# Attention scores of two key heads in one chain, their products interleaved by half of the array

## The chip, the cores and the metric

One core of a Trainium2 chip. The metric is the device time of one execution in microseconds; the time of a kernel is the median of its runs.

## What is computed

Two layers of a decoder trunk over 256 tokens of width 1024. Each layer has a gated feed-forward block, a mixing block of two branches that add up, a second feed-forward block and a small embedding block. The change is in the attention branch of the mixing block: 16 query heads and 4 key heads of width 64, a window of 128 keys, one sink logit a head. Cut to what matters:

```python
q, k = head_rmsnorm(a_q), head_rmsnorm(a_k)
scores = einsum("bnqhgd,bnkhd->bnhgqk", q, windows(k)) * 64 ** -0.5
scores = where(band & valid, scores, -inf)
mx = maximum(max(scores, axis=-1), sink)
pr = exp(scores - mx)
den = sum(pr, axis=-1) + exp(sink - mx)
ha = einsum("bnhgqk,bnkhd->bnqhgd", pr / den, windows(v))
h = h + (sigmoid(g_m) * (hm @ w_branch_m) + sigmoid(g_a) * (ha @ w_branch_a)) @ w_out
```

## The kernel before

**Precision by splitting.** Every matmul operand is a pair: a rounded part `hi`, cast by ScalarE, and the rest `lo`, subtracted by VectorE (`splitting`, L466). A product is three matmuls: hi x hi, hi x lo, lo x hi. All weights go this way: `raw` comes by DMA, `wh` and `wl` are its two parts, in a ring of 8 slots that TensorE gives back as it uses them up (`feed`, L328).

**Jobs and chains.** The matmuls with weights are jobs that run one after the other. In a mixing block they are `kvq` (keys, values and queries of the attention), `v`, `gt` (a gate), `if` (input and forget gates), `ya` (the attention's output by `w_branch_a`), then those of the other branch. All other work runs in chains: Python generators whose steps are put between the matmuls of the jobs (`tick`, L196). A planner's clock (`Clock`, L60) estimates when a step's inputs are ready, and a chain goes on when TensorE's estimated time has come to that. TensorE, ScalarE, VectorE and SyncE execute their instructions in the order that this writes; a later instruction doesn't overtake a waiting one.

**Attention.** Key heads are handled by two pairs p; g = 0 and 1 are the two key heads of a pair, whose 64 rows lie in partitions 0 to 63 and 64 to 127. `groups` (L1171) starts one chain `group` (L1184) for each p, each block t of 128 queries and each g, at most five at once. A chain does the following. A mask goes into a PSUM bank `sc` by a matmul of the full array (identity times `band`, 512 columns). On top go the score products: S = 128 (t = 0) or 256 keys (t = 1), stationary a 64 x 128 tile of `qT`, moving a 64 x S tile of `kT`. A bank holds four heads for t = 0 and two for t = 1, that is twelve or six products; t = 1 takes two banks in turn. VectorE takes the maxima `mx` (a reduction and a small step), ScalarE the exponentials `pr` with their sums `dn`. Then come `es`, the reciprocal, the scaling of `pr`, and for each block of keys four transposes into a bank `tp`, its split into `ptd`, and three matmuls `ha` (output by values). The last chain of a p and t splits `ha` into `haT`, which shares its tiles with `qT`, so the profile shows this as `qT<-ha`.

**Who waits for it.** `ya` starts when all chains have been started (L797 passes `finish(groups[0])`). It runs over the first half of `haT` (p = 0) for both halves of the output, 96 matmuls, and then over the second half (p = 1), another 96. Ahead of each step it finishes the chains that write what it reads (`XT.wait`, L158), both t. Beside it runs the chain `scans`, with VectorE steps on `gates`, five transposes of `gates` into a `tp` bank, and their copy `gcols`.

**Banks.** PSUM has eight banks; all of `kvq`, `v`, `gt`, `ya`, `sc`, `tp`, `ha` are tiles of one pool (L184). A new tile that is given a bank waits for the last reader of the tile that had it.

Of the kernel before, what the change touches and what calls it, by code (L numbers as in the profile page):

```python
# [14 lines left out]
AF = mybir.ActivationFunctionType  # L15
ALU = mybir.AluOpType
AX = mybir.AxisListType
PSUM = bass.MemoryType.PSUM

P = 128  # L20
# [10 lines left out]
AQ, AKV, AD = 16, 4, 64  # L31
# [6 lines left out]
ACTIVE = 5  # L38
# [125 lines left out]
class Trunk:  # L164
# [561 lines left out]
    def mix(self, l, xT, sink):  # L726
# [15 lines left out]
        def before():  # L742
            self.feature_columns()
            att.begin()
            groups.append(self.later(att.groups(groups)))
# [351 lines left out]
class Swa:  # L1097
# [73 lines left out]
    def groups(self, chains):  # L1171
        tr, acc = self.tr, {}
        for p in range(2):
            for t in range(NT):
                while any(self.inputs.get(i, tr) is tr or self.inputs[i] in tr.bg
                          for i in [(0, s) for s in range(t + 1)] + [(p + 1, t)]):
                    yield
                for g in range(2):
                    while sum(c in tr.bg for c in chains) > ACTIVE:
                        yield  # L1180
                    chains.append(tr.start(self.group(t, p, g, acc)))
                    self.haT.written(chains[-1], 4 * p, 4, t)

    def group(self, t, p, g, acc):  # L1184

        tr, nc = self.tr, self.nc
        S = (t + 1) * P
        per = NB // S
        rows = slice(g * AD, (g + 1) * AD)
        tok = slice(t * P, (t + 1) * P)  # L1190
        hd = slice(4 * (2 * p + g), 4 * (2 * p + g) + 4)
        pr = tr.slot("pr")[:, : 4 * S].rearrange("p (j s) -> p j s", j=4)
        mx, den, es = tr.col("mx", 4), tr.col("dn", 4), tr.col("es", 4)

        def scores(j0):
            ps = tr.bank("sc").rearrange("p (j s) -> p j s", j=per)
            mask = tr.band[:, 2 * P - S :]
            nc.tensor.matmul(ps, tr.identb, mask[:, None, :].to_broadcast([P, per, S]), start=True, stop=False,
                             skip_group_check=True)
            for j in range(per):  # L1200
                for x, y in ((0, 0), (0, 1), (1, 0)):
                    nc.tensor.matmul(ps[:, j, :], self.qT[x](4 * p + j0 + j, tok, p=rows), self.kT[rows, y, p, :S],
                                     start=False, stop=x == 1, skip_group_check=True)
            return ps

        def weights(j0, ps):
            js = slice(j0, j0 + per)
            nc.vector.tensor_reduce(mx[:, js], ps, axis=AX.X, op=ALU.max)
            nc.vector.scalar_tensor_tensor(mx[:, js], mx[:, js], -0.125, self.nsink[:, hd][:, js], op0=ALU.mult,
                                           op1=ALU.min)  # L1210
            yield
            for j in range(per):
                i = j0 + j
                nc.scalar.activation(pr[:, i, :], ps[:, j, :], AF.Exp, scale=0.125, bias=mx[:, i : i + 1],
                                     accum_out=den[:, i : i + 1])

        for j0 in range(0, 4, per):
            ps = scores(j0)
            yield
            yield from weights(j0, ps)  # L1220
        nc.vector.tensor_tensor(es, mx, self.sink[:, hd], op=ALU.add)
        yield
        nc.scalar.activation(es, es, AF.Exp)
        yield
        nc.vector.tensor_tensor(den, den, es, op=ALU.add)
        nc.vector.reciprocal(den, den)
        yield
        for j in range(4):
            nc.scalar.mul(pr[:, j, :], pr[:, j, :], den[:, j : j + 1])
        yield  # L1230
        total = 2 * (t + 1)
        for s in range(t + 1):
            ps = tr.bank("tp")
            for j in range(4):
                nc.tensor.transpose(ps[:, j * P : (j + 1) * P], pr[:, j, s * P : (s + 1) * P], tr.ident)
            yield
            ptd = tr.slot("ptd", F32R)[:, : 2 * NB].rearrange("p (x n) -> p x n", x=2)
            yield from tr.splitting(ptd[:, 0], ptd[:, 1], ps)
            yield
            if (t, p) not in acc:  # L1240
                acc[t, p] = [tr.bank("ha"), 0]
            out, n = acc[t, p]
            acc[t, p][1] += 1
            tr.mm3(out, self.vpad[s, 0][:, 2 * p + g, :], self.vpad[s, 1][:, 2 * p + g, :], ptd[:, 0], ptd[:, 1],
                   n == 0, n == total - 1)
        if n == total - 1:
            yield
            yield from tr.splitting(self.haT[0](4 * p, tok, 4), self.haT[1](4 * p, tok, 4),
                                    out.rearrange("p (j t) -> p j t", j=4))
# [28 lines left out]
```

## Time and profile before

| | us |
|---|---|
| runs before: median (lowest to highest of 3) | 1404.9 (1402.35 to 1405.91) |
| the profiled execution | 1401.73 |
| its span, first to last instruction | 1400.0 |
| TensorE busy in it | 1384.3 |
| VectorE busy | 863.0 |
| ScalarE busy | 727.8 |

Granted TensorE clock over the span: 0.999 of full. Matmuls are pipelined: a record of one lasts longer than its share of the engine, and the next starts before it ends. The pace is read from start to start, or from how many lie in a stretch. L130 stands for nearly all instructions, since one helper records them all; tiles tell them apart. `sc<-band` is a mask, `sc<-kT,qT` a score product.

### The profile page before, as it was taken

Reading aid. Unit: us, or ns where it says so; the run is one execution under the profiler, and the core shown is the slowest. Engines: PE = TensorE matmul, PEld = TensorE weight load, DVE = VectorE, ACT = ScalarE, POOL = GpSimd, SP = SyncE. Lnnn points to the kernel's source line nnn. Section 1 sums busy time; section 2 is a strip of 40 time slices with the busy share of each in tenths; the row PEclk is TensorE's granted clock in tenths of the full one; section 3 lists DMA queues with packets and bytes.
Section 4 is the critical chain, followed back from the end, with each engine's and each line's share of the span. In section 5 each row is a group of like instructions: output and inputs, shape, how many; then the busy total and the mean of one; then the engine's idle time right before and its main releaser. Section 6 shows DMA issues by size and latency. Waiting matters only on the chain.

```text
span 1400.0 us, 21954 instructions
## 1 busy us (share of the span) xinstructions
PE 1384.3 (99%) x9056; PEld 1249.0 (89%) x9056; DVE 863.0 (62%) x1213; ACT 727.8 (52%) x1138; POOL 53.8 (4%) x84
## 2 busy tenths in 40 slices
PE   8999999999999999999999999999999999999998
PEld 6999887899899889988879998878998998999886
DVE  5655457656886665454565554586668876554544
ACT  5554346765665454443554443467656654444433
POOL 0000012000000000000000000120000000000000
PEclk9999999999999999999999999999999999999999
DMA  6665645355545565565456566443545544755651
GB/s 210 221 206 172 219 147 182 107 135 169 177 151 181 166 204 188 166 232 181 149 172 210 178 198 212 143 145 117 151 151 196 175 158 161 220 190 182 203 180 60
DMA packets 125830, 243.81 MB, mean 174 GB/s; under 512 B 14977, under 2 KB 23841, under 8 KB 125730
## 3 DMA queue, kind: packets, MB, share of 16 engines
q1 hardware_dynamic: 125730, 242.41, 54.2%
q8 instruction: 71, 1.16, 0.3%
q14 instruction: 29, 0.24, 0.1%
HBM read 241.34 MB, written 1.05 MB: 173 GB/s over the span
## 4 chain that ended last, share of the span: by engine, by line
PE 93%; DMA 3%; DVE 2%; ACT 1%; issue 1%; POOL 0%; SPq 0%; ACTq 0%; POOLq 0%
PE dn L130 16%; PE pg L130 15%; PE pu L130 14%; PE gt L130 7%; PE z L130 7%; PE gu L130 6%; PE kvq L130 5%; PE ya L130 3%; PE v L130 3%; PE ym L130 3%; PE og L130 3%; PE yo L130 3%; PE tp L130 3%; PE sc L130 2%; DMA raw<-in_ffn_w_gate_dram 1%; PE ha L130 1%
## 5 line engine op out<-in xcount | busy, mean ns | idle before, releaser
L130 DVE TENSOR_TENSOR wl<-raw,wh 128x1024 fp32r<-128x1024 f32 (+1 forms) x448 | 541.5, 1222 | 372.8 <-ACT wh L130 369.3
L130 ACT CAST wh<-raw 128x1024 fp32r<-128x1024 f32 x448 | 461.8, 1049 | 432.7 <-PE dn L130 88.4
L130 PE MATMUL dn<-wh,hid 128*128 128x512 f32 x688 | 217.9, 395 | 0.0
L130 PE MATMUL pg<-uT,wh 128*128 128x256 f32 x1088 | 194.6, 282 | 0.0
L130 PE MATMUL pu<-uT,wh 128*128 128x256 f32 x1088 | 193.6, 281 | 0.0
L130 PEld LDWEIGHTS pg<-uT,wh 128*128 128x128 f32 x1088 | 167.1, 189 | 0.2
L130 PEld LDWEIGHTS pu<-uT,wh 128*128 128x128 f32 x1088 | 166.9, 189 | 0.0
L130 PEld LDWEIGHTS dn<-wh,hid 128*128 128x128 f32 x688 | 129.3, 188 | 29.8
L130 PE MATMUL pg<-uT,wl 128*128 128x256 f32 x544 | 153.2, 282 | 0.0
L130 PE MATMUL pu<-uT,wl 128*128 128x256 f32 x544 | 153.1, 281 | 0.0
L130 PE MATMUL dn<-wl,hid 128*128 128x512 f32 x352 | 139.1, 395 | 0.0
L130 PEld LDWEIGHTS pu<-uT,wl 128*128 128x128 f32 x544 | 102.7, 189 | 0.0
L130 PEld LDWEIGHTS pg<-uT,wl 128*128 128x128 f32 x544 | 102.6, 189 | 0.0
L130 PE MATMUL gt<-uT,wh 128*128 128x256 f32 x512 | 93.7, 284 | 0.0
L130 PE MATMUL z<-uT,wh 128*128 128x256 f32 x512 | 92.3, 282 | 0.0
L130 PE MATMUL gu<-wh,uT 128*128 128x512 f32 x256 | 84.3, 406 | 1.2 <-ACT uT L130 1.2
L130 PEld LDWEIGHTS gt<-uT,wh 128*128 128x128 f32 x512 | 79.0, 189 | 1.2
L130 PEld LDWEIGHTS dn<-wl,hid 128*128 128x128 f32 x352 | 66.2, 188 | 15.1
L130 PEld LDWEIGHTS z<-uT,wh 128*128 128x128 f32 x512 | 78.7, 189 | 0.2
L130 PE MATMUL z<-uT,wl 128*128 128x256 f32 x256 | 72.1, 282 | 0.0
L130 PE MATMUL gt<-uT,wl 128*128 128x256 f32 x256 | 72.0, 281 | 0.0
L130 PE MATMUL kvq<-wh,uT 128*128 128x512 f32 x192 | 63.7, 402 | 0.0
(194 smaller groups left out, 2061.5 us busy)
## 6 DMA issues: line engine op xcount, KB each, us to landing
raw<-in_w_in_dram SPq DMA_DIRECT2D x60, 1024.0 KB, 5.1
raw<-in_ffn_w_up_dram SPq DMA_DIRECT2D x40, 1024.0 KB, 5.1
raw<-in_ffn_w_down_dram SPq DMA_DIRECT2D x40, 1024.0 KB, 5.2
raw<-in_ffn_w_gate_dram SPq DMA_DIRECT2D x39, 1024.0 KB, 5.7
raw<-in_w_branch_a_dram SPq DMA_DIRECT2D x16, 512.0 KB, 6.0
raw<-in_w_branch_m_dram SPq DMA_DIRECT2D x8, 1024.0 KB, 5.0
raw<-in_w_out_dram SPq DMA_DIRECT2D x8, 1024.0 KB, 5.1
raw<-in_ple_gate_w_dram SPq DMA_DIRECT2D x8, 1024.0 KB, 6.6
```

The costliest lines, as they stand in the source:

```text
L130: return issue(*args, **kw)
```

## The change

`group` is cut in two. `scores` does for both g of a p and t what stood ahead of `es`: two banks at once, both masks, then the products in turn, one of g = 0 (rows 0 to 63), one of g = 1 (rows 64 to 127), each into its own bank; then the maxima of both, then the exponentials of both. At its end it adds two chains `outputs`, one for each g, which do the rest as before. `groups` starts a pair when fewer than five chains run, the chain `groups` itself being one of them (before: a single chain when at most five run); the pair's chain counts as two.

```diff
--- before.py
+++ after.py
@@ -1175,49 +1175,53 @@
                 while any(self.inputs.get(i, tr) is tr or self.inputs[i] in tr.bg
                           for i in [(0, s) for s in range(t + 1)] + [(p + 1, t)]):
                     yield
-                for g in range(2):
-                    while sum(c in tr.bg for c in chains) > ACTIVE:
-                        yield
-                    chains.append(tr.start(self.group(t, p, g, acc)))
-                    self.haT.written(chains[-1], 4 * p, 4, t)
-
-    def group(self, t, p, g, acc):
+                while sum(c in tr.bg for c in chains) >= ACTIVE:
+                    yield
+                chains += 2 * [tr.start(self.scores(t, p, acc, chains))]
+                self.haT.written(chains[-1], 4 * p, 4, t)
+
+    def scores(self, t, p, acc, chains):
+
 
         tr, nc = self.tr, self.nc
         S = (t + 1) * P
         per = NB // S
-        rows = slice(g * AD, (g + 1) * AD)
         tok = slice(t * P, (t + 1) * P)
-        hd = slice(4 * (2 * p + g), 4 * (2 * p + g) + 4)
-        pr = tr.slot("pr")[:, : 4 * S].rearrange("p (j s) -> p j s", j=4)
-        mx, den, es = tr.col("mx", 4), tr.col("dn", 4), tr.col("es", 4)
-
-        def scores(j0):
-            ps = tr.bank("sc").rearrange("p (j s) -> p j s", j=per)
-            mask = tr.band[:, 2 * P - S :]
-            nc.tensor.matmul(ps, tr.identb, mask[:, None, :].to_broadcast([P, per, S]), start=True, stop=False,
-                             skip_group_check=True)
+        rows = [slice(g * AD, (g + 1) * AD) for g in range(2)]
+        hd = [slice(4 * (2 * p + g), 4 * (2 * p + g) + 4) for g in range(2)]
+        pr = [tr.slot("pr")[:, : 4 * S].rearrange("p (j s) -> p j s", j=4) for _ in range(2)]
+        mx, den = ([tr.col(n, 4) for _ in range(2)] for n in ("mx", "dn"))
+        mask = tr.band[:, None, 2 * P - S :].to_broadcast([P, per, S])
+        for j0 in range(0, 4, per):
+            js = slice(j0, j0 + per)
+            ps = [tr.bank("sc").rearrange("p (j s) -> p j s", j=per) for _ in range(2)]
+            for g in range(2):
+                nc.tensor.matmul(ps[g], tr.identb, mask, start=True, stop=False, skip_group_check=True)
             for j in range(per):
                 for x, y in ((0, 0), (0, 1), (1, 0)):
-                    nc.tensor.matmul(ps[:, j, :], self.qT[x](4 * p + j0 + j, tok, p=rows), self.kT[rows, y, p, :S],
-                                     start=False, stop=x == 1, skip_group_check=True)
-            return ps
-
-        def weights(j0, ps):
-            js = slice(j0, j0 + per)
-            nc.vector.tensor_reduce(mx[:, js], ps, axis=AX.X, op=ALU.max)
-            nc.vector.scalar_tensor_tensor(mx[:, js], mx[:, js], -0.125, self.nsink[:, hd][:, js], op0=ALU.mult,
-                                           op1=ALU.min)
+                    for g in range(2):
+                        nc.tensor.matmul(ps[g][:, j, :], self.qT[x](4 * p + j0 + j, tok, p=rows[g]),
+                                         self.kT[rows[g], y, p, :S], start=False, stop=x == 1, skip_group_check=True)
             yield
-            for j in range(per):
-                i = j0 + j
-                nc.scalar.activation(pr[:, i, :], ps[:, j, :], AF.Exp, scale=0.125, bias=mx[:, i : i + 1],
-                                     accum_out=den[:, i : i + 1])
-
-        for j0 in range(0, 4, per):
-            ps = scores(j0)
+            for g in range(2):
+                nc.vector.tensor_reduce(mx[g][:, js], ps[g], axis=AX.X, op=ALU.max)
+                nc.vector.scalar_tensor_tensor(mx[g][:, js], mx[g][:, js], -0.125, self.nsink[:, hd[g]][:, js],
+                                               op0=ALU.mult, op1=ALU.min)
             yield
-            yield from weights(j0, ps)
+            for g in range(2):
+                for j in range(per):
+                    i = j0 + j
+                    nc.scalar.activation(pr[g][:, i, :], ps[g][:, j, :], AF.Exp, scale=0.125, bias=mx[g][:, i : i + 1],
+                                         accum_out=den[g][:, i : i + 1])
+        for g in range(2):
+            chains.append(tr.later(self.outputs(t, p, g, acc, hd[g], pr[g], mx[g], den[g])))
+            self.haT.written(chains[-1], 4 * p, 4, t)
+
+    def outputs(self, t, p, g, acc, hd, pr, mx, den):
+
+        tr, nc = self.tr, self.nc
+        tok = slice(t * P, (t + 1) * P)
+        es = tr.col("es", 4)
         nc.vector.tensor_tensor(es, mx, self.sink[:, hd], op=ALU.add)
         yield
         nc.scalar.activation(es, es, AF.Exp)
```

What stands in the queues, at three places of the first layer (the second layer has the same).

TensorE at the first scores, p = 0, t = 0, before (`qT_136` is the hi part, `qT_138` the lo part):

```order
L130 MATMUL kvq_2225<-wh_2144,uT_117 128x512
L130 MATMUL kvq_2225<-wl_2145,uT_117 128x512
L130 MATMUL kvq_2225<-wh_2144,uT_119 128x512
L130 LDWEIGHTS identb
L130 MATMUL sc_2315<-band,identb 128x512
L130 MATMUL sc_2315<-kT_1996,qT_136 128x128 x2
L130 MATMUL sc_2315<-kT_1996,qT_138 128x128
```

and after the change:

```order
L130 MATMUL kvq_2225<-wh_2144,uT_119 128x512
L130 LDWEIGHTS identb
L130 MATMUL sc_2317<-band,identb 128x512
L130 LDWEIGHTS identb
L130 MATMUL sc_2318<-band,identb 128x512
L130 MATMUL sc_2317<-kT_1996,qT_136 128x128
L130 MATMUL sc_2318<-kT_1996,qT_136 128x128
```

Twelve products into one bank have become 24 that change bank, and half of the array, at each step, behind two masks.

TensorE inside `ya`, before (`qT_136` and `qT_138` are the first half of `haT`, `qT_137` and `qT_139` the second):

```order
L130 MATMUL ya_3185<-qT_136,wh_2953 128x256
L130 MATMUL ya_3185<-qT_138,wh_2953 128x256
L130 MATMUL ya_3185<-qT_136,wl_2954 128x256
L130 MATMUL ha_3082<-ptd_3208,vpad_1994 128x512 x3
L130 MATMUL ya_3186<-qT_136,wh_2953 128x256
L130 MATMUL ya_3186<-qT_138,wh_2953 128x256
L130 MATMUL ya_3186<-qT_136,wl_2954 128x256
```

and after:

```order
L130 MATMUL ya_3165<-qT_136,wl_2990 128x256
L130 MATMUL ha_3229<-ptd_3253,vpad_1994 128x512 x3
L130 MATMUL ha_3229<-ptd_3255,vpad_1994 128x512 x3
L130 MATMUL tp_3340<-ident,gates_3159 128x4
L130 MATMUL tp_3340<-ident,gates_3158 128x4
L130 MATMUL tp_3340<-ident,gates_3159 128x4
L130 MATMUL tp_3340<-ident,gates_3160 128x4 x2
L130 MATMUL ya_3162<-qT_137,wh_3013 128x256
L130 MATMUL ya_3162<-qT_139,wh_3013 128x256
```

The last `ha` stood inside the first half of `ya`, with 54 matmuls of that half behind it. Now the last two stand at its end, and behind the transposes of `gates` comes the first matmul of the second half.

VectorE at the same place, before:

```order
L130 TENSOR_SCALAR nM_3184<-gates_3183 4x256
L130 TENSOR_SCALAR nM_3184<-gates_3183 4x128
L130 TENSOR_TENSOR wl_3241<-raw_3104,wh_3240 128x1024
L130 TENSOR_TENSOR qT_139<-ha_3082,qT_137 128x4x128
L130 TENSOR_TENSOR wl_3303<-raw_3104,wh_3302 128x1024
L130 TENSOR_TENSOR rows_93<-nM_3184,rows_93 4x384
L130 TENSOR_TENSOR wl_3313<-raw_3211,wh_3312 128x1024
L130 TENSOR_TENSOR wl_3338<-raw_3211,wh_3337 128x1024
L130 COPY gcols_3368<-tp_3353 128x20
```

and after:

```order
L130 TENSOR_SCALAR nM_3161<-gates_3160 4x128
L130 TENSOR_TENSOR ptd_3253<-tp_3233,ptd_3253 128x512
L130 TENSOR_TENSOR ptd_3255<-tp_3241,ptd_3255 128x512
L130 TENSOR_TENSOR wl_3301<-raw_3097,wh_3300 128x1024
L130 TENSOR_TENSOR rows_93<-nM_3161,rows_93 4x384
L130 TENSOR_TENSOR wl_3311<-raw_3221,wh_3310 128x1024
L130 COPY gcols_3346<-tp_3340 128x20
L130 TENSOR_TENSOR wl_3337<-raw_3221,wh_3336 128x1024
L130 TENSOR_TENSOR qT_139<-ha_3229,qT_137 128x4x128
L130 TENSOR_TENSOR wl_3391<-raw_3320,wh_3390 128x1024
```

The subtraction `qT<-ha` stood two places behind `nM`, with `gcols` five places later. Now `gcols` and one `wl` stand ahead of it.

TensorE at the last scores, p = 1, t = 1, inside `gt`, before:

```order
L130 MATMUL gt_2754<-uT_116,wh_2496 128x256
L130 MATMUL gt_2754<-uT_118,wh_2496 128x256
L130 MATMUL gt_2754<-uT_116,wl_2497 128x256
L130 LDWEIGHTS identb
L130 MATMUL sc_2849<-band,identb 128x512
L130 MATMUL sc_2849<-kT_1996,qT_137 128x256 x2
L130 MATMUL sc_2849<-kT_1996,qT_139 128x256
```

and after:

```order
L130 MATMUL tp_2921<-ident,pr_2636 128x128 x4
L130 MATMUL gt_2719<-uT_116,wh_2579 128x256
L130 MATMUL gt_2719<-uT_118,wh_2579 128x256
L130 MATMUL gt_2719<-uT_116,wl_2580 128x256
L130 MATMUL gt_2719<-uT_116,wh_2579 128x256
L130 MATMUL gt_2719<-uT_118,wh_2579 128x256
L130 MATMUL gt_2719<-uT_116,wl_2580 128x256
L130 LDWEIGHTS identb
L130 MATMUL sc_2939<-band,identb 128x512
L130 LDWEIGHTS identb
L130 MATMUL sc_2940<-band,identb 128x512
```

One mask has become two in a row. In the built program `sc_2939` has the bank of the transposes `tp_2908`, which stand six `gt` matmuls further up, and `sc_2940` that of `tp_2921`, the transposes shown. Before, six `gt` matmuls and an `ha` stood ahead of the mask, and no transposes.

## Rows read from the trace of the kernel before

**Rows 1.** The page: the busy time of TensorE and the shares of the chain that ended last, by engine and by line:

```profile
PE 1384.3 (99%) x9056; PEld 1249.0 (89%) x9056; DVE 863.0 (62%) x1213; ACT 727.8 (52%) x1138; POOL 53.8 (4%) x84
...
PE 93%; DMA 3%; DVE 2%; ACT 1%; issue 1%; POOL 0%; SPq 0%; ACTq 0%; POOLq 0%
PE dn L130 16%; PE pg L130 15%; PE pu L130 14%; PE gt L130 7%; PE z L130 7%; PE gu L130 6%; PE kvq L130 5%; PE ya L130 3%; PE v L130 3%; PE ym L130 3%; PE og L130 3%; PE yo L130 3%; PE tp L130 3%; PE sc L130 2%; DMA raw<-in_ffn_w_gate_dram 1%; PE ha L130 1%
```

**Rows 2.** The waits of TensorE over the whole run: who waited for whom, us in total, times, the longest. No wait of over 0.15 us is listed between 228 and 340 us:

```profile
PE tp L130 <- DVE xn L130: 4.0, 2, 2.5
...
PE tp L130 <- DVE wl L130: 1.6, 1, 1.6
...
PE tp L130 <- DVE sg L130: 1.0, 1, 1.0
```

**Rows 3.** Groups of ScalarE's instructions from 228 to 340 us (the attention stage of the first layer): line, engine, operation, tiles, shapes, count, then busy us, mean ns, idle us before them and what ended it:

```profile
L130 ACT CAST wh<-raw 128x1024 fp32r<-128x1024 f32 x28 | 29.3, 1053 | 12.4 <-DMA raw<-in_w_in_dram 5.0 <-PE ya L130 4.8 <-PE gt L130 1.3
```

**Rows 4.** TensorE in order of time around the first score blocks: start us, us to the last end, engine, line, operation, tiles, shapes, count:

```profile
233.46 0.39 PE L130 MATMUL kvq<-wh,uT 128*128 128x512 f32 x1
233.69 0.39 PE L130 MATMUL sc<-band,identb 128*128 128x512 bf16 x1
234.01 1.55 PE L130 MATMUL sc<-kT,qT 64*128 64x128 f32 x12
235.49 0.39 PE L130 MATMUL sc<-band,identb 128*128 128x512 bf16 x1
235.81 1.55 PE L130 MATMUL sc<-kT,qT 64*128 64x128 f32 x12
237.29 0.50 PE L130 MATMUL kvq<-wh,uT 128*128 128x512 f32 x1
...
238.10 0.39 PE L130 MATMUL sc<-band,identb 128*128 128x512 bf16 x1
238.42 0.97 PE L130 MATMUL sc<-kT,qT 64*128 64x256 f32 x6
239.32 0.39 PE L130 MATMUL sc<-band,identb 128*128 128x512 bf16 x1
```

**Rows 5.** The instructions that write or read the tile `sc`: count, duration in ns (min/median/max), first and last start in us, shapes:

```profile
L130 PEld LDWEIGHTS sc<-kT,qT x192: 182/187/192, 234.0 to 982.1; 64*128 64x128 f32 x192
L130 PE MATMUL sc<-kT,qT x192: 268/275/389, 234.0 to 982.3; 64*128 64x128 f32 x96, 64*128 64x256 f32 x96
...
L130 PE MATMUL sc<-band,identb x24: 389/390/391, 233.7 to 981.2; 128*128 128x512 bf16 x24
```

**Rows 6.** The instructions on the tile `gates`, the same columns: the loads of its five tiny transposes:

```profile
L130 PEld LDWEIGHTS tp<-ident,gates x10: 133/136/138, 326.6 to 1019.8; 4*128 4x128 f32 x10
```

**Rows 7.** TensorE's loads in order of time at the first of these transposes:

```profile
326.57 0.39 PEld L130 LDWEIGHTS tp<-ident,gates 4*128 4x128 f32 x5
```

**Rows 8.** TensorE in order of time inside `ya`: the last `ha`, then `ya` and the transposes of `gates`:

```profile
318.00 0.86 PE L130 MATMUL ha<-ptd,vpad 128*128 128x512 f32 x3
318.70 0.40 PE L130 MATMUL ya<-qT,wh 128*128 128x256 f32 x2
...
326.13 0.40 PE L130 MATMUL ya<-qT,wh 128*128 128x256 f32 x2
326.36 0.28 PE L130 MATMUL ya<-qT,wl 128*128 128x256 f32 x1
326.57 0.47 PE L130 MATMUL tp<-ident,gates 4*128 4x4 f32 x5
326.98 0.51 PE L130 MATMUL ya<-qT,wh 128*128 128x256 f32 x2
```

**Rows 9.** ScalarE in order of time in the same stretch: the cast that begins the split of `ha`; a cast of `ptd` has the same shape (in brackets idle us before and what ended it):

```profile
318.90 0.59 ACT L130 CAST qT<-ha 128x512 fp32r<-128x512 f32 x1 [1.33 <-PE ha L130]
```

**Rows 10.** VectorE in order of time in the same stretch:

```profile
315.60 0.69 DVE L130 TENSOR_TENSOR ptd<-tp,ptd 128x512 fp32r<-128x512 f32 x1
...
321.45 0.67 DVE L130 TENSOR_TENSOR qT<-ha,qT 128x512 fp32r<-128x512 f32 x1
...
326.23 1.23 DVE L130 TENSOR_TENSOR wl<-raw,wh 128x1024 fp32r<-128x1024 f32 x1 [1.14 <-ACT wh L130]
327.38 0.17 DVE L130 COPY gcols<-tp 128x20 f32<-128x20 f32 x1
```

**Rows 11.** TensorE in order of time at four transposes ahead of a long matmul:

```profile
230.02 0.60 PE L130 MATMUL tp<-ident,qn 128*128 128x128 f32 x4
230.38 0.48 PE L130 MATMUL kvq<-wh,uT 128*128 128x512 f32 x1
230.70 0.40 PE L130 MATMUL kvq<-wl,uT 128*128 128x512 f32 x1
```

**Rows 12.** TensorE in order of time around its longest wait:

```profile
699.92 0.40 PE L130 MATMUL pg<-wh,uT 128*128 128x512 f32 x1
702.79 1.82 PE L130 MATMUL tp<-ident,xn 128*128 128x128 f32 x8 [2.48 <-DVE xn L130]
```

**Rows 13.** Busy time of the engines (instructions) in three stretches, then the granted TensorE clock, the DMA share and GB/s; the third holds a wait of 1.0 us for `sg`:

```profile
702.00:704.00 2.00, 1.21 (x7) 1.11 (x8) 1.40 (x3) 0.93 (x3) 0.00 (x0) 0.75 0.00 0
704.00:707.50 3.50, 3.50 (x13) 2.90 (x12) 1.38 (x2) 3.23 (x5) 0.00 (x0) 0.66 0.02 5
...
509.00:512.00 3.00, 1.96 (x16) 1.67 (x15) 2.62 (x3) 2.34 (x4) 0.00 (x0) 1.00 0.25 98
```

## The prediction

> **What bounds the kernel now.** I read the page first. TensorE is busy for 1384.3 of 1400.0 us, and 93% of the chain that ended last is its matmuls, with the score products `sc` at 2% of the span [rows 1]. The reader is to see an engine that hardly ever stops, so time goes only where its queue gets shorter or where it is made to wait. Then the waits: TensorE's own are few, the largest kind 4.0 us over the whole run, and none of them lies in the attention stage; weights cost it one wait of 1.6 us [rows 2]. In that stretch ScalarE, which prepares the weights, waits for TensorE to give slots back (4.8 us behind `ya`, 1.3 us behind `gt`) [rows 3]. Weights are not late there, and a faster TensorE finds them ready. Last I read the score blocks one by one. A mask matmul of 512 columns takes 0.32 us to the next start, against 0.23 us for the 512-column matmul ahead of it; twelve products of 128 columns take 1.48 us, six of 256 columns 0.90 us [rows 4]. Over two layers there are 96 products of each width and 24 masks [rows 5]. One product of 128 columns lasts 0.275 us and twelve lie in 1.55 us, so they follow each other at (1.55 - 0.275) / 11 = 0.116 us; a 256-column matmul of the full array follows at 0.40 - 0.28 = 0.12 us [rows 4, 5, 8]. That 128 columns take as long as 256 says that the load of the stationary tile sets the pace of the short ones: its record is 0.187 us long, and these loads overlap [rows 5].
>
> **The change on TensorE.** The products stay 192 and the masks 24; none is added. Two things go. First, the score blocks now come in 12 pairs. The step from a full-array mask to half-array products costs 0.32 - 0.23 = 0.09 us, and what entering and leaving cost beyond the pace is 1.48 - 12 x 0.116 = 0.09 us for the narrow block and 0.90 - 6 x 0.12 = 0.18 us for the wide one [rows 4]. A pair pays each once instead of twice. Second, every product on rows 0 to 63 is followed by one on rows 64 to 127 into another bank. If the two halves of the array load and stream side by side, a pair takes the time of one.
>
> No row shows two half-array products in flight on different halves, so I bound the pair. It can't take less than one product alone, 0.116 us. Two records can't follow faster than the shortest pace in the trace: five tiny transposes, whose load record is 0.136 us, lie in 0.39 us, that is (0.39 - 0.136) / 4 = 0.064 us each, 0.127 us for two [rows 6, 7]. At the other end nothing overlaps, 0.232 to 0.24 us. I take 0.127: loads already run while the matmul before them is in flight [rows 5], so the engine's parts do work side by side, and the two halves share neither rows of the array nor a bank.
>
> Narrow pair (t = 0; 2 per layer, 4 in all): now 237.29 - 233.69 = 3.60 us [rows 4]. After: masks 0.23 + 0.32, twelve pairs x 0.127 = 1.52, entering and leaving 0.09, sum 2.16. Gain 1.44 x 4 = 5.8 us. Wide pair (t = 1; 4 per layer, 8 in all): now 2 x (239.32 - 238.10) = 2.44 us. After: 0.55 + 6 x 0.127 + 0.18 = 1.49. Gain 0.95 x 8 = 7.6 us. Sum 13.4 us off TensorE's queue, all of it on the path. With no overlap the masks' part alone is left: (3.60 - 3.42) x 4 + (2.44 - 2.17) x 8 = 2.9 us. These are the two ends.
>
> In the Trainium skill, "TensorE: Matmul & The Clock Gate", section "Part 3: Packing small matmuls", has matmuls on separate row groups start some 4 ns apart, with a gain of 3.07 for four. By it a pair would cost 0.116 + 0.004 = 0.12 us, and the sum would be 14.0 in place of 13.4; no run here shows it.
>
> **The change on the other engines.** Reductions, exponentials, casts and weight steps keep number and size. They stand in another order, and the exponentials of a pair come in one run. The cover is the slack above: TensorE waits for nobody in this stage [rows 2]. If that cover were gone, a late weight would cost the 1.2 us of one `wl` step [rows 10]. `es` and the outputs start one round of the planner later; that delay I don't price by itself, since it comes out at two places.
>
> Place one, inside `ya`. `ya` reads the first half of `haT` for 96 matmuls, then the second. Now the last `ha` stands 54 `ya` matmuls ahead of the switch, 54 x 0.12 = 6.5 us, and its split hides under them. In the changed order six `ha` matmuls stand right at the switch, with five `gates` transposes behind them, and the next `ya` reads the tile just made. From TensorE's first free slot after `ha` (318.70 in the trace), ScalarE's cast starts 0.20 later and takes 0.59 [rows 8, 9]. VectorE's queue, though, has the copy `gcols` and one `wl` ahead of the subtraction. `gcols` waits for the transposes, 0.47 us; it holds the queue for some 0.1, the `wl` 1.15 (from 326.23 to the next start at 327.38), the subtraction 0.67 [rows 8, 10]. With 0.05 of handover that is 2.44 us; TensorE would be free at 0.41 [rows 8]. It stands 2.0 us, twice: 4.0 us. If the `wl` were no hindrance, it would be 0.20 + 0.59 + 0.67 + 0.05 - 0.41 = 1.1; if the cast or the `wl` come a microsecond late, 3.0. Queued behind it on TensorE is all the rest of `ya`.
>
> Place two, inside `gt`. The second wide score pair of the last key pair writes its second mask into the bank of the transposes `tp` that stand six `gt` matmuls ahead. That bank is free when ScalarE and VectorE have split it. From the transposes' start: 0.60 to their end, 0.59 cast, 0.68 subtraction, 0.05 handover, 1.92 us [rows 8 to 11]. TensorE reaches the mask after 0.36 + 0.09 [rows 11] + 6 x 0.12 + 0.23 = 1.40. Wait 0.5 us, twice: 1.0 us. Bounds 0 and 1 us each.
>
> The Trainium skill, "TensorEngine Tiling (Array Packing)", section "Gotcha 1: PSUM Pressure", says that row tiles need several banks at once. This speaks against the change at place two, and the order of the queues agrees; by that page alone the price stays open.
>
> Sum: -13.4 + 4.0 + 1.0 = -8.4 us. The profiled execution took 1401.7 us (its span 1400.0), so 1393.3 on its own scale. The three timed runs before lie at 1402.4 to 1405.9, median 1404.9, some 3 us above it; a median is what will be compared, so I forecast **1396.5 us**. Bounds of this case: pair cost 0.116 and both waits at their least give -14.2 + 2.2 = -12.0 (1393). The waits at their most give -13.4 + 8 = -5 (1400). One more thing can hang on the wait in `ya`: after an idle of 2.48 us the granted clock stood at 0.75 and 0.66 of full, a fall to the lower of its two levels for part of the stretch, and cost about 0.34 x 3.5 + 0.25 x 2 = 1.7 us; after an idle of about 1 us it stayed at 1.00 [rows 12, 13]. A wait of 2.0 lies between; at worst 3.4 us for both layers.
>
> **Rivals.** (1) *No overlap*: the halves take turns, because loads of both halves go through one path. For it: in the trace the load sets the pace of narrow products [rows 5]. Against: the halves share no row. Then only the masks' 2.9 us go, and the waits come: -2.9 + 5.0 = +2.1, 1407 us. (2) *Half*: streams overlap, loads in part: -8.2 + 5.0 = -3.2, 1402 us. (3) *Turning costs*: each change of half drains the array as the step from mask to products does, 0.09 us. There are 23 changes in each of 4 narrow pairs and 11 in each of 8 wide ones, 180 x 0.09 = 16.2: -2.9 + 16.2 + 5.0 = +18, 1423 us. With no overlap, 12 ns a change are enough to be slower by over 0.3% ((4.2 - 2.1) / 180). For it: the only switch of array form that the trace has costs this much [rows 4]; against: both halves have one form. By the Trainium skill, "TensorEngine Tiling (Array Packing)", section "Key Properties", a change of mode drains the engine and a change of tile does not, which would make this rival's price nothing.
>
> **How the numbers follow.** 0.3% is 4.2 us; less can't be told from no change. Chances: forecast 0.60, no overlap 0.18, half 0.13, turning costs 0.09. Faster by over 0.3% (under 1400.7): 0.52 of the 0.60, 0.04 of the half; 0.56. Same: 0.08 + 0.09 + 0.13 = 0.30. Slower: 0.05 of no overlap (clock falls too) and 0.09; 0.14. The range leaves out the turning costs (0.09), the top of no overlap (0.04) and the lowest tail of the forecast (0.05): 1393 to 1409. The forecast's own range is 1393 to 1402.
>
> **What would show it.** Right: a row of 24 `sc` products of 128 columns in about 1.6 us and 12 of 256 in about 0.95; a TensorE wait of some 2 us per layer at the first `ya` after `gates`, ended by VectorE's `qT`, and one of 0.5 us at an `sc` mask. Wrong: rows of 2.8 us (no overlap) or above 3 (turning costs), a wait in `ya` over 3 us or none, or waits on `wl` in the attention stage.

## The result, and the profile after

| | before | after |
|---|---|---|
| median of 5 runs, us | 1404.9 | 1392.64 |
| lowest to highest | 1399.91 to 1406.12 | 1390.64 to 1395.02 |
| ratio, 95% interval | | 0.9917 [0.9895, 0.9938] |
| the profiled execution, its span | 1401.73, 1400.0 | 1395.02, 1393.2 |

The changed kernel is faster: by 12.3 us from median to median, by 11.7 by the ratio (8.7 to 14.8). Forecast were 8.4 us and 1396.5, with a range of 1393 to 1409; the median lies 0.4 us below its lower end, and by the ratio, 1404.9 x 0.9917 = 1393.2, it lies just inside. First the page: the span, the busy time, and the chain that ended last, by engine.

```profile
span 1393.2 us, 21942 instructions
...
PE 1371.4 (98%) x9056; PEld 1236.9 (89%) x9056; DVE 862.3 (62%) x1213; ACT 726.7 (52%) x1138; POOL 55.0 (4%) x84
...
PE 90%; DMA 3%; DVE 3%; ACT 2%; issue 1%; POOL 0%; SPq 0%; ACTq 0%; POOLq 0%
```

Against [rows 1] the number of instructions on TensorE and VectorE is the same, TensorE is busy for 12.9 us less, and its share of the chain went from 93 to 90% while VectorE's went from 2 to 3: some of what the queue lost came back as waiting. Where it was lost, the timeline of TensorE at the first two score pairs of the changed kernel shows, beside [rows 4]:

```profile
233.85 0.60 PE L130 MATMUL sc<-band,identb 128*128 128x512 bf16 x2
234.39 1.55 PE L130 MATMUL sc<-kT,qT 64*128 64x128 f32 x24
235.87 0.50 PE L130 MATMUL kvq<-wh,uT 128*128 128x512 f32 x1
...
236.68 0.60 PE L130 MATMUL sc<-band,identb 128*128 128x512 bf16 x2
237.22 0.97 PE L130 MATMUL sc<-kT,qT 64*128 64x256 f32 x12
238.12 0.50 PE L130 MATMUL v<-wh,uT 128*128 128x512 f32 x1
```

Twenty-four products lie in the 1.55 us in which twelve lay, and twelve wide ones in the 0.97 of six. A narrow pair now takes 235.87 - 233.85 = 2.02 us (3.60 before), a wide one 238.12 - 236.68 = 1.44 (2.44). Where it came back, the list of TensorE's waits shows; these three were not in [rows 2]:

```profile
PE ya L130 <- DVE qT L130: 2.7, 2, 1.3
...
PE sc L130 <- DVE ptd L130: 0.9, 2, 0.5
...
PE ya L130 <- ACT qT L130: 0.6, 2, 0.3
```

They are 4.2 us in all. The whole list grew from 10.4 us to 16.8; the other 2.2 come mainly from the start of the feed-forward block, `gu`, which waits for VectorE's `wl` (1.5 us, new) and for ScalarE's `uT` (1.9 in place of 1.2), and from `qn` (0.6) and `wif` (0.4), less one of 1.0 for `sg` that is gone. The wait for `uT` differs as much between the profiles of the experiments, from 0.7 to 1.9.

TensorE in order of time at the switch of `ya` to the second half of `haT`, and ScalarE and VectorE in the same stretch, which answer to [rows 8, 9, 10]:

```profile
317.29 1.56 PE L130 MATMUL ha<-ptd,vpad 128*128 128x512 f32 x6
318.78 0.47 PE L130 MATMUL tp<-ident,gates 4*128 4x4 f32 x5
319.52 0.38 PE L130 MATMUL ya<-qT,wh 128*128 128x256 f32 x1 [0.28 <-ACT qT L130]
321.25 0.39 PE L130 MATMUL ya<-qT,wh 128*128 128x256 f32 x1 [1.34 <-DVE qT L130]
```

```profile
318.88 0.58 ACT L130 CAST qT<-ha 128x512 fp32r<-128x512 f32 x1 [0.46 <-PE ha L130]
...
319.28 0.18 DVE L130 COPY gcols<-tp 128x20 f32<-128x20 f32 x1 [1.63 <-PE tp L130]
319.38 1.22 DVE L130 TENSOR_TENSOR wl<-raw,wh 128x1024 fp32r<-128x1024 f32 x1
320.51 0.68 DVE L130 TENSOR_TENSOR qT<-ha,qT 128x512 fp32r<-128x512 f32 x1
```

VectorE stands idle for 1.63 us, takes the copy, then a whole `wl`, and only then the subtraction for which TensorE waits. One product of the high part goes ahead at 319.52, since it needs ScalarE's cast alone. Counted against a TensorE without waits: five transposes cost 326.98 - 326.57 = 0.41 [rows 8], so `ya` could start at 318.78 + 0.41 = 319.19 and its second product 0.12 later, at 319.31. That one starts at 321.25, 1.94 us late; from `ya`'s free start to the same record it is 2.06.

The second place, TensorE at the last wide pair of the layer:

```profile
284.89 0.39 PE L130 MATMUL sc<-band,identb 128*128 128x512 bf16 x1
285.73 0.38 PE L130 MATMUL sc<-band,identb 128*128 128x512 bf16 x1 [0.45 <-DVE ptd L130]
286.03 0.98 PE L130 MATMUL sc<-kT,qT 64*128 64x256 f32 x12
286.94 0.50 PE L130 MATMUL gt<-uT,wh 128*128 128x256 f32 x2
```

The second mask waits for the bank of the transposes. The pair takes 286.94 - 284.89 = 2.05 us in place of 1.44, so the wait costs 0.61, of which the profile puts 0.45 down to `ptd`.

Last the clock. Windows of the changed kernel behind the wait in `ya` (busy time of the engines, then granted clock, DMA share, GB/s):

```profile
319.00:322.30 3.30, 1.68 (x14) 1.29 (x13) 1.91 (x3) 1.96 (x3) 0.00 (x0) 1.00 0.58 179
322.30:325.70 3.40, 3.40 (x18) 3.40 (x17) 0.00 (x0) 0.88 (x3) 0.00 (x0) 0.50 0.76 287
325.70:328.00 2.30, 2.30 (x22) 2.20 (x21) 0.89 (x1) 1.83 (x4) 0.00 (x0) 1.00 0.00 0
```

For 3.40 us the clock stood at half, 1.2 GHz, behind a stretch in which TensorE was busy for 1.68 of 3.30 us. Half of 3.4 us, 1.7, is lost. The second layer has the same fall at 1011.8 us. The fall after the long wait for `xn`, which the profiled execution before had [rows 13], is not in this one.

### The profile page after: what moved, and what is told of

Same layout as the page of the kernel before. It is cut to its first block, busy times and chain, and to the rows that moved or that the text cites. A ratio compares the mean times of both kernels' runs of the same rounds, so it can differ in the third digit from the quotient of the medians.

```text
span 1393.2 us, 21942 instructions
## 1 busy us (share of the span) xinstructions
PE 1371.4 (98%) x9056; PEld 1236.9 (89%) x9056; DVE 862.3 (62%) x1213; ACT 726.7 (52%) x1138; POOL 55.0 (4%) x84
## 4 chain that ended last, share of the span: by engine, by line
PE 90%; DMA 3%; DVE 3%; ACT 2%; issue 1%; POOL 0%; SPq 0%; ACTq 0%; POOLq 0%
PE dn L130 16%; PE pg L130 15%; PE pu L130 14%; PE gu L130 7%; PE z L130 7%; PE gt L130 6%; PE ya L130 4%; PE ym L130 3%; PE v L130 3%; PE og L130 3%; PE yo L130 3%; PE kvq L130 3%; PE tp L130 2%; PE sc L130 1%; DVE wl L130 1%; PE ha L130 1%
```

## The experiments

All start from the changed kernel, and only what the diff shows differs: e1 to e4 and e8 change what stands in TensorE's queue (e3 also which banks the maxima and exponentials read together), e5 to e7 how many chains may run at once. Runs were made in two groups, each beside runs of the kernel before: e1 to e4 (before: median 1401.5, 25 runs), e5 to e8 (before: 1405.95, 11 runs). Ratios are against the kernel before of the same group. The theories to part were: (A) the halves of the array work side by side, (B) the gain comes from fewer steps between masks and products and from the new order of the chains, (C) it comes from the change of bank between neighbours.

**e1, the halves one after the other.** The same two masks and products, first all of g = 0, then all of g = 1.

```diff
-            for j in range(per):
-                for x, y in ((0, 0), (0, 1), (1, 0)):
-                    for g in range(2):
+            for g in range(2):
+                for j in range(per):
+                    for x, y in ((0, 0), (0, 1), (1, 0)):
```

> The changed kernel, with all products of the first half of the array ahead of all of the second in each pair of banks; queues otherwise the same. Theory A (the two halves of the array load and stream side by side when neighbours in the queue lie on different halves): the overlap goes and only the shared masks stay; 24 narrow products and two masks take about 3.4 us instead of 2.0, 12 wide ones 2.2 instead of 1.44, 1.4 x 4 + 0.75 x 8 = 11.5 us in all, so about 1404 us. Theory B (the gain comes from fewer masks steps and from the new order of the chains): no change, 1392.6 us.

1399.18 us (10 runs), 0.9967 [0.9949, 0.9984]. TensorE at the first two pairs:

```profile
233.42 2.51 PE L130 MATMUL sc<-kT,qT 64*128 64x128 f32 x24
...
237.19 1.32 PE L130 MATMUL sc<-kT,qT 64*128 64x256 f32 x12
```

The narrow products take 2.51 in place of 1.55 us, the wide ones 1.32 in place of 0.97. So the order of the products is what counts, and masks and chains are not. (The alternation of banks is gone here as well; e3 parts it from that of the halves.) But less is lost than by no overlap, so the expected 1404 us were not reached: 24 at the pace of 0.116 would be 23 x 0.116 + 0.275 = 2.94 us, and e3 below has twelve wide ones without overlap at 1.69. The difference, 0.43 and 0.37 us, is three to four products. At the one boundary between the halves the first products of the second half start beside the last of the first. The records of single products tell how far ahead that is. The first product on a half has a longer record than those behind it (0.32 us for 128 columns, 0.38 for 256). The second half's first one is the tenth of its block to start in all four narrow pairs, 6 to 7 ns behind the ninth, and the fourth in all eight wide ones. In the queue it stands thirteenth and seventh, so it starts beside a product four places ahead of it.

**e2, runs of three.** For each head the three products of g = 0, then the three of g = 1.

```diff
             for j in range(per):
-                for x, y in ((0, 0), (0, 1), (1, 0)):
-                    for g in range(2):
+                for g in range(2):
+                    for x, y in ((0, 0), (0, 1), (1, 0)):
```

> The changed kernel with the halves changing after every three products (one head's) instead of after each. Theory A, where only neighbours in the queue overlap: of 24 narrow products 7 stand at a change of half and run beside the one ahead of them, so 17 x 0.116 + masks and steps = 2.6 us a narrow pair and 9 x 0.12 + 0.18 + 0.55 = 1.8 us a wide one, 5 us more than the changed kernel in all, about 1398 us. If the engine looks far enough ahead to fill the other half from three places on, no loss: 1392.6. Theory B: no loss either, but then the serial kernel shows none.

1392.33 us (4 runs), 0.9926 [0.9903, 0.9948]: as the changed kernel. TensorE at the first two pairs:

```profile
233.69 1.56 PE L130 MATMUL sc<-kT,qT 64*128 64x128 f32 x24
...
236.53 0.98 PE L130 MATMUL sc<-kT,qT 64*128 64x256 f32 x12
```

Nothing is lost, 1.56 and 0.98 us. My theory that only neighbours in the queue overlap fell. Products three places apart pair up as well, with starts mostly 9 to 11 ns apart against mostly 2 to 5 in the changed kernel. With e1 this bounds how far the engine reaches: four products ahead at the boundary, and not six, since the first products of a wide pair in e1 run alone.

**e3, two banks of one half.** For t = 1 a pair is made of the two banks of one g, so that banks alternate and the half doesn't; t = 0 stays as changed.

```diff
+        todo = [[(g, j0) for g in range(2)] for j0 in range(0, 4, per)]
+        if t:
+            todo = [[(g, j0) for j0 in range(0, 4, per)] for g in range(2)]
...
-                    for g in range(2):
-                        nc.tensor.matmul(ps[g][:, j, :], self.qT[x](4 * p + j0 + j, tok, p=rows[g]),
-                                         self.kT[rows[g], y, p, :S], start=False, stop=x == 1, skip_group_check=True)
+                    for i, (g, j0) in enumerate(two):
+                        nc.tensor.matmul(ps[i][:, j, :], self.qT[x](4 * p + j0 + j, tok, p=rows[g]),
+                                         self.kT[rows[g], y, p, :S], start=False, stop=x == 1, skip_group_check=True)
```

> The changed kernel with another pairing for t = 1: the two banks of one key head are interleaved, so neighbours lie in different banks but on the same half of the array; t = 0 as in the changed kernel. Theory A: wide pairs go back to about 2.17 us from 1.44, 8 x 0.73 = 5.8 us, about 1398.5 us. Rival C (it is the change of bank, not of half, that lets products overlap): wide pairs stay at 1.44, 1392.6 us.

1398.25 us (10 runs), 0.9968 [0.9952, 0.9985]. TensorE at the first narrow and the first wide pair:

```profile
234.31 1.55 PE L130 MATMUL sc<-kT,qT 64*128 64x128 f32 x24
...
236.61 0.60 PE L130 MATMUL sc<-band,identb 128*128 128x512 bf16 x2
237.15 1.69 PE L130 MATMUL sc<-kT,qT 64*128 64x256 f32 x12
238.76 0.50 PE L130 MATMUL v<-wh,uT 128*128 128x512 f32 x1
```

The narrow pairs, left alone, overlap; the wide ones, with the same alternation of banks, don't: 1.69 against 0.97 us. Theory C is out: with banks in alternation and the half unchanged, nothing overlaps. The pair takes 238.76 - 236.61 = 2.15 us against 2.44 before, so the part that masks and a single entry save is 0.29 us, where the prediction had 2.44 - 2.17 = 0.27.

**e4, each mask ahead of its own products.** The chains of the changed kernel, the TensorE blocks of the kernel before.

```diff
             for g in range(2):
                 nc.tensor.matmul(ps[g], tr.identb, mask, start=True, stop=False, skip_group_check=True)
-            for j in range(per):
-                for x, y in ((0, 0), (0, 1), (1, 0)):
-                    for g in range(2):
+                for j in range(per):
+                    for x, y in ((0, 0), (0, 1), (1, 0)):
```

> The changed kernel's chains, with each bank's mask right ahead of its own products and no interleaving, as the kernel before had it. Theory A: all of the gain in the queue goes, 3.60 and 2.44 us a pair, 14.3 us in all, and the waits in ya and at the mask stay: about 1407 us, a little slower than the kernel before. Against the serial kernel that is 2.9 us for the shared masks. Theory B: the part of the gain that is due to the chains' order stays.

1408.31 us (10 runs, 1403.48 to 1416.33), 1.004 [1.0015, 1.0065]: slower than before. Its blocks of products are those of [rows 4] again, 12 in 1.55 and 6 in 0.97 us, and TensorE at the switch of `ya` has the wait of the changed kernel:

```profile
325.02 0.47 PE L130 MATMUL tp<-ident,gates 4*128 4x4 f32 x5
325.76 0.38 PE L130 MATMUL ya<-qT,wh 128*128 128x256 f32 x1 [0.28 <-ACT qT L130]
327.49 0.38 PE L130 MATMUL ya<-qT,wh 128*128 128x256 f32 x1 [1.35 <-DVE qT L130]
```

So this is the price of the new chains by itself. Of theory B the chains' order is out, since with it alone nothing of the gain is left; the steps between masks and products are worth the 0.29 us a wide pair of e3. The mask doesn't wait here, since 0.97 us of products now lie ahead of it. Its clock was lower than that of the other kernels (mean 0.990 to 0.998), with a fall of 10.2 us at 932.7 too, far from `ya`, for which I have no cause. Its three runs at 0.998 took 1403.5 to 1404.9, the four of the kernel before at 0.998 1400.3 to 1402.3: near 3 us more, against the two waits' 4.

**e5, e6, e7, more chains at once.** `ACTIVE` from 5 to 6, 7 and 9; a pair starts when fewer chains than that run. TensorE's score blocks stay; pairs start sooner.

```diff
-ACTIVE = 5
+ACTIVE = 6
```

> The changed kernel with ACTIVE = 6, so that a pair starts with one more chain running; the last ha then stands ahead of ya, 96 ya matmuls and more from the matmul that reads it. If the wait in ya is the queue's order (ha, gates, one weight step, subtraction) and nothing else: the 2.07 us wait and the fall of the clock behind it are gone in both layers, 4.1 us and 1.6 us for each fall, so 1386 to 1388 us against 1392.6. Rival: the attention's work is late anyway and TensorE waits at another place, for ptd or for pr: no gain, 1392.6, with new waits on PE.

> ACTIVE = 7, two pairs of chains more in flight than in the changed kernel's plan near v: the last ha stands still earlier in gt. Same gain as with 6 if only the wait in ya counts (1386 to 1388 us). If more chains cost something (exponentials in front of the casts of weights or of v, banks held longer), it shows as new waits of TensorE on DVE or ACT and 1388 to 1392 us.

> ACTIVE = 9: all four pairs start as soon as their queries are there, inside v. Banks are the limit now. If eight banks are enough, 1386 to 1388 us; if score banks and those of v hold each other up, waits of TensorE at sc or v of 0.5 to 2 us each and 1388 to 1394 us.

| | us | ratio |
|---|---|---|
| e5 (6) | 1388.14, 4 runs | 0.9882 [0.9864, 0.9901] |
| e6 (7) | 1395.76, 6 runs | 0.9935 [0.9918, 0.9952] |
| e7 (9) | 1392.02, 6 runs | 0.9909 [0.9893, 0.9926] |

With 6, the last `ha` stands ahead of `if` and `ya`, with the `if` matmuls and the whole first half of `ya` for its split to hide under. Neither `ya` nor `sc` is among the waits of TensorE, and the window over the stage shows no idle time:

```profile
300.00:335.00 35.00, 35.00 (x293) 34.20 (x292) 24.46 (x38) 22.23 (x36) 0.00 (x0) 1.00 0.63 182
```

This version beats both kernels: all four of its runs (1386.08 to 1388.93) lie below all five of the changed kernel. With 7 and 9 the wait in `ya` is gone too, but TensorE waits at another place, for the split of `wif`; 1395.76 us lie above both ranges that were expected of e6. The waits of TensorE in e6:

```profile
PE if L130 <- DVE wif L130: 6.2, 2, 3.1
...
PE tp L130 <- DVE v L130: 0.7, 2, 0.3
```

and in e7:

```profile
PE if L130 <- DVE wif L130: 2.2, 2, 1.3
...
PE tp L130 <- ACT pr L130: 1.5, 2, 0.8
```

The attention's work isn't what holds up `wif`: its last splits are done by 304 us, and VectorE stands idle ahead of `wif` in e6. ScalarE's casts of `wif` stand behind the cast of a weight that hasn't landed yet, in e6 and in e7:

```profile
305.97 1.04 ACT L130 CAST wh<-raw 128x1024 fp32r<-128x1024 f32 x1 [2.51 <-DMA raw<-in_w_branch_a_dram]
306.92 0.33 ACT L130 CAST wif<-wif 128x32 fp32r<-128x32 f32 x2
...
307.17 0.31 DVE L130 TENSOR_TENSOR wif<-wif,wif 128x32 fp32r<-128x32 f32 x2 [3.28 <-ACT wif L130]
```

```profile
304.29 1.99 ACT L130 CAST wh<-raw 128x1024 fp32r<-128x1024 f32 x2 [3.48 <-DMA raw<-in_w_branch_a_dram]
306.19 0.33 ACT L130 CAST wif<-wif 128x32 fp32r<-128x32 f32 x2
```

In e5 the casts of `wif` stand behind such a cast too, which waits for its weight for 1.09 us, but six `ha` and six `gt` matmuls are still ahead of `if`, and TensorE doesn't wait. In e6 the clock fell to half for 3.41 us behind both of these waits, in e7 behind neither.

**e8, the wait filled.** Eight extra mask matmuls into a bank that nobody reads, at the switch of `ya`; nothing is left out.

```diff
                         xT.wait(kk, *range(NT))
                         self.need(part)
+                        if (base, kk, u, c) == ("ya", KT // 2, 0, 0):
+                            fill = self.bank("fill").rearrange("p (j s) -> p j s", j=2)
+                            for _ in range(8):
+                                self.tc.nc.tensor.matmul(fill, self.identb, self.band[:, None, :].to_broadcast([P, 2, 2 * P]),
+                                                         start=True, stop=True, skip_group_check=True)
```

> The changed kernel with eight more mask matmuls of 512 columns into an unread bank at the place of the wait in ya, 8 x 0.22 = 1.8 us that fit into the 2.07 us. If the idle of TensorE is what lets its clock fall behind it: no fall at 320 to 330 and at 1010 to 1020 us, and up to 1.6 us a layer less than the changed kernel, 1390 to 1392 us; the wait itself stays in length. If the clock falls for another reason, it falls as before and the time stays at 1392.6 us.

1390.73 us (5 runs), 0.9902 [0.9884, 0.992]. TensorE there, and the windows of the same stretch:

```profile
319.08 0.47 PE L130 MATMUL tp<-ident,gates 4*128 4x4 f32 x5
319.48 1.90 PE L453 MATMUL fill<-band,identb 128*128 128x512 bf16 x8
321.03 0.91 PE L130 MATMUL ya<-qT,wh 128*128 128x256 f32 x2
```

```profile
320.00:325.00 5.00, 4.95 (x38) 3.85 (x36) 1.50 (x2) 2.36 (x6) 0.00 (x0) 1.00 0.72 238
325.00:330.00 5.00, 5.00 (x46) 4.81 (x44) 3.04 (x4) 3.46 (x8) 0.00 (x0) 1.00 0.05 20
```

TensorE does 1.55 us of useless work where it idled, and the clock stays at full. The profiles of the changed kernel and of e1 to e4 have the wait in ten layers, and a fall behind it in eight; e5 and e8 have no such idle time in four layers, and no fall there. As far as fourteen layers can show it, the fall hangs on the idle time. It doesn't follow each time: of the waits of 2.5 to 3.0 us for `xn` at about 700 us, which nine of the ten profiles have, four had a fall behind them. The time of e8 by itself doesn't settle this, since the intervals of 0.9902 and of the changed kernel's 0.9917 overlap.

## Why the prediction came out

**The pair of products: right in kind, a little short in size.** The forecast took 0.127 us for two products on different halves, from two tiny transposes, which no record seemed to undercut. The premise, that two records can't follow faster than the shortest pace in the trace, was wrong: the two of a pair start mostly 2 to 5 ns apart, and 8 at most. Measured: twelve pairs lie in 1.55 us where twelve single products did, so a pair costs what one product costs, (1.55 - 0.275) / 11 = 0.116 us, the lower end of the bounds. A narrow pair took 2.02 (forecast 2.16), a wide one 1.44 (1.49). Four narrow pairs, six wide and the two that wait make 4 x 2.02 + 6 x 1.44 + 2 x 2.05 = 20.8 us in place of 4 x 3.60 + 8 x 2.44 = 33.9. Without the two waits, 0.6 each, the queue is 14.3 us shorter, where 13.4 were forecast. This term of the sum was mis-sized. The row chosen was a poor neighbour: the five transposes all use the same four rows of the array, so their pace bounds what one part does, and not what two do together (this is argued, no run tried it). By the 4 ns between starts that the Trainium skill, "TensorE: Matmul & The Clock Gate", section "Part 3: Packing small matmuls", states, the estimate was 14.0; the trace agrees with both numbers, with its 2 to 5 ns and 14.3 us.

**The rivals fell by the rows that the prediction had named.** No overlap wanted rows of 2.8 us, turning costs above 3; the row is 1.55. A half overlap would lie between 1.55 and 2.8, and nothing of the 1.55 is left for it. e1 and e3 show that overlap is the cause, and not another effect of the new order: beside e2 of the same group (1392.33), the kernel that takes it from all pairs but for the boundary is 6.9 us longer, the one that takes it from the wide pairs alone 5.9. By the rows the first should be 4 x 0.95 + 8 x 0.35 = 6.6, the second 8 x (1.69 - 0.97) = 5.8.

**Place one: right.** Forecast 2.0 us a layer, ended by VectorE's `qT`, with `gcols` and one `wl` ahead of it; measured 1.9 to 2.1, with these in this order. Each term can be read: cast at 318.88 for 0.58, `wl` 1.13 to the next start, subtraction 0.68. **Place two: right.** Forecast 0.5, measured 0.45 by the list of waits and 0.6 by the length of the pair.

**The weights: right in the outcome, thin in the reading.** That weights are not late was read from ScalarE's waits for slots in [rows 3]. The same row has a larger entry, 5.0 us in which ScalarE waited for weights to land, and the prediction passes over it. It cost TensorE nothing in this stage, where no wait on `wl` is listed; e6 and e7 show what it costs when a small cast that TensorE needs soon stands behind such a weight.

**The clock: named, but not in the sum.** The forecast left the fall behind `ya` as a possible extra of 1.7 us a layer. It came in both layers of the profiled execution, 1.7 each. Set against the profiled times: -14.3 + 2 x 2.0 + 2 x 0.6 = -9.1; two falls of 1.7 are added and the one of [rows 13] is gone, +1.7; that is -7.4, and the spans differ by -6.8. The waits elsewhere, 2.2 us more than before, are not in this sum; with them it is -5.2, so it closes to some 2 us and not better.

**What is left of the size.** The ratio gives 11.7 us, not 8.4 or 9.1. Of the difference, 0.9 is the pair. The rest, 2.6, lies within the interval, and goes with the clock of single runs, since the runs of one kernel lie apart by what clock they were granted: those of the kernel before in the two groups took 1398.9 to 1402.2 us at a mean of 0.999 to 1.000 (14 runs, median 1401.0) and 1403.9 to 1409.5 at 0.992 to 0.996 (17 runs); the two of the changed kernel at 0.999 and 1.000 took 1391.15 and 1390.64. At equal clock that is a gain of about 10 us, near the sum of 9.1, though the runs are of different groups. Where the kernel before loses its clock in its longer runs no trace here shows, so this part stays open. The range's lower end had the pair at its least and the waits near theirs, on top of the first median; it left no room for a before that had lost more clock in its median run than in the profiled one, which would put the time just below the range, as it came out; that this is the reason isn't shown.

**Where the rest of the gain went.** Of 14.3 us, 5.2 went into the two waits, and e5 shows it from the other side: without them the ratio gives 1404.9 x (1 - 0.9882) = 16.6 us, against 11.7. That is 2.3 us more than the 14.3 of the queue, so the ratio of e5 holds about the same unexplained surplus as the 2.6 above.

## What to carry to other kernels

Products that fill half of the array's rows can be put in twos, one on each half and each into its own bank: here, with 128 and 256 columns, two took the time of one. Two in one bank no run tried. The order needn't be strict, since runs of three did as well as single steps, but runs of six and of twelve lost half of the overlap or more (0.35 of 0.72 us, 0.96 of 1.39). What a shorter queue gains is then at risk wherever a chain's last step now stands closer to its reader; one more chain in flight gave the waits back here, and with two or four more, what another reader needed stood behind a weight that hadn't landed.

## What the runs showed of the hardware

- TensorE starts a product of the other half ahead of earlier products of the first one: e2 lost nothing with runs of three, and e1 gained three to four products at its one boundary, where the second half's first product starts beside one four places ahead of it. So for products on different halves it doesn't hold that TensorE keeps to the written order, as the section on the kernel before has it. The Trainium skill, "TensorE: Matmul & The Clock Gate", section "Part 3: Packing small matmuls", says that matmuls keep the order of the queue in start and end. In that order, runs of three would let only the last of one run and the first of the next go together, 17 steps for 24 products, 16 x 0.116 + 0.275 = 2.13 us. The row is 1.56, and the measured row decides.
- Two loads of 64 rows by 128 columns, one for each half, go on together: single loads last 0.187 us and follow each other every 0.116 us on one half [rows 4, 5], and two halves do this at once: in the changed kernel the loads of two halves start mostly 3 to 4 ns apart. So the pace of loads that [rows 5] suggested as a bound is one for each half.
- The granted clock fell to half for 3.41 us behind TensorE's wait in `ya` (0.28 and 1.34 us idle) in eight of ten layers, and in neither of the two layers of e8, where useless matmuls filled that wait.
